# New order tables, filler tables and scheduler preferences for the attention half of a two-layer trunk

## The chip, the cores and the metric

The kernel runs on one core of a Trainium2 chip. The metric is the device time of one execution in microseconds (us); the smaller the better. TensorE (PE) does matrix products and transposes, VectorE (DVE) and ScalarE (ACT) work on tiles in SBUF and PSUM, GpSimd (POOL) helps DVE, and SyncE (SP) issues the DMAs. A difference under 0.5% (6.3 us here) is one that a measurement of this kernel does not tell from none.

## What is computed

Two layers, each an attention half and a feed-forward half on 512 tokens of width 1024, in float32:

```
h = rms_norm(x, attn_norm[l]);  proj = h @ w_in[l]
o_fox  = forgetting attention, 6 heads x 64:  softmax(q.k/8 + c[t] - c[s]) v
o_diff = differential attention, 4 heads:     (softmax(q1 k1) - lam softmax(q2 k2)) v, then rms_norm
o_dsa  = sparse attention, 6 heads x 64:      an indexer scores all keys, the top 128 of each row stay
x = x + concat(o_fox, o_diff, o_dsa) @ w_out[l]
h = rms_norm(x, ffn_norm[l]);  gate, up = split(h @ w_gate_up[l])
x = x + (silu(gate) * up) @ w_down[l]
```

All attention is causal. Every projection is made as three products (high x high, low x high, high x low) of operands split into a high part rounded to fp32r and a remainder.

## The kernel before

The attention half of a layer runs through 16 heads in one list: four differential heads (names with d), six forgetting heads (f), six sparse heads (s). A name reads kind, layer, pair of heads, head in the pair: f0_2_0 is layer 0, third pair of forgetting heads, first head. A head goes through stages: its queries and keys are transposed (tp_q, tp_k; ACT copies them out as T_q, T_k), scores are multiplied (s_), DVE adds the bias and takes the row minimum (x_ and st_, line 444, "ttr"), ACT takes the exponential (p_, line 445), PE transposes the weights (t_, line 456), ACT and DVE copy them out as high and low part (pt0 line 470, pt1 line 474), PE multiplies them with the values (o_), and at the end of a pair the rows are divided by their sums (osb, lines 513 and 518) and split (oh by ACT, ol by DVE).

The loop over rounds works on several heads at once: a round holds eleven stages, those of the scores of the next head, the transposes of this one, the products with the values of the last one. ORDER gives the order of the eleven in each round, a hexadecimal digit for each. After each stage, FILL says how many units of other PE work follow. A unit is taken from one queue (`fillers`): 12 matmuls of the projection chunks (pj), then 6 matmuls of the output projection of the differential heads (wo_diff), then 9 of the forgetting heads (wo_fox), then the sparse ones. SEARCH says how many steps of the top-128 search (DVE, lines 880 and 881) follow; INDEX_FILL does the same as FILL ahead of the first round.

PE runs in program order, so ORDER and FILL are its order. On DVE, ACT and POOL a scheduler sets the order at build time; `ahead(kind)` gives the instructions of a kind a preference, by the numbers in AHEAD (a larger one puts them further forward, a negative one back). At run time each engine takes its instructions strictly in the order so found; an instruction that waits for a semaphore holds up all behind it on its engine. PSUM tiles come from rings: "mm" three buffers (projections), "st" four (scores and transposes), "o" one. A matmul into a ring's buffer waits until the last reader of the tile before it there is done.

After the attention half, `split_input` (line 186 on) makes yh (ACT, line 192) and yl (DVE, line 195) of x for the feed-forward half; the first gate-and-up product gu0_0_0 (lines 958 to 960) takes them one by one.

```
for e, si in enumerate(ORDER[r + 1]):
    stages[int(si, 16)]()
    step(filler, int(FILL[r + 1][e]))
    if r <= 8:
        step(topk, int(SEARCH[r + 1][e]))
```

Of the kernel before, what the change touches and what calls it, by code (L numbers as in the profile page):

```python
# [17 lines left out]
P = 128  # L18
# [3 lines left out]
KT = D // P  # L22
# [9 lines left out]


ORDER = [
    "025314678a9", "0213457869a", "0213564789a", "1023647589a", "0312547698a", "1023465798a",
    "012435687a9", "0214365789a", "3021475698a", "0132645798a", "0123564879a", "021364587a9",
    "0132546798a", "1032546789a", "102345768a9", "103624758a9", "012345689a7", "012436587a9",
    "0362145897a",
]
FILL = [  # L40
    "10100011102", "01011000210", "10000011011", "01000011200", "00411000001", "00011010011",
    "02000002011", "00200040001", "00010101000", "10000000001", "00000000000", "01100000010",
    "00000000010", "00000000001", "00000000010", "00000000110", "00000000000", "00010100000",
    "01000000000",
]
SEARCH = [
    "00000000300", "00002010000", "00000000002", "11100004000", "00002000020", "00100000010",
    "00002001000", "20101020101", "01100001001", "02501140001",
]
INDEX_FILL = "03210121000201021"  # L50

AHEAD = {
    "bias": 300, "comb": 60, "dqh": -150, "dql": 150, "evac": 1000, "norm": 150, "oadd": 600, "osb": 60,
    "prep": 200, "raw": 300, "red": -150, "rl": 1000, "rope": 60, "rows": -60, "rt": 60, "sc": 1000,
    "split": -60, "sq": 200, "stack": 60, "tl": 300, "topk": 150, "ttr": 1000, "val": 300, "vall": 1000,
    "wl": 200, "yh": 300, "yl": 250, "ssq": -100, "post": 1000, "wh": 0, "fh": 200, "xadd": 1000,
}


# [29 lines left out]
def trunk(ctx: ExitStack, tc: tile.TileContext, x_in, w_in, w_out, w_gu, w_dn, vecs, gfeat, rope, out):  # L89
    nc = tc.nc  # L90
    V, A, G, T, SY = nc.vector, nc.scalar, nc.gpsimd, nc.tensor, nc.sync
# [17 lines left out]
    ahead = lambda kind: tc.high_priority(AHEAD[kind])  # L109
# [29 lines left out]
    dram = ctx.enter_context(tc.tile_pool(name="dram", bufs=1, space=bass.MemoryType.DRAM))  # L139


    def weights(src, n, step, name, eng=V, load=None, hi="wh"):

        raw = wp.tile([P, 1024], F32, tag="raw", name=f"raw_{name}", bufs=2)
        for o in range(0, n, load or n):
            SY.dma_start(raw[:, o:o + (load or n)], src[:, o:o + (load or n)])
        piece = n if n <= 512 else -(-n // step // 2) * step
        hs, ls = [], []
        for o in range(0, n, piece):
            w = min(piece, n - o)  # L150
            h = wp.tile([P, 512], F32R, tag="wh", name=f"wh_{name}_{o}")
            with ahead(hi):
                A.activation(h[:, :w], raw[:, o:o + w], AF.Copy)  # L153
            lo = wp.tile([P, 512], F32R, tag="wl", name=f"wl_{name}_{o}")
            with ahead("wl"):
                eng.tensor_tensor(lo[:, :w], raw[:, o:o + w], f32(h[:, :w]), op=ALU.subtract)  # L156
            hs.append(h)
            ls.append(lo)

        def part(a, b):  # L160
            e = a // piece
            return hs[e][:, a - e * piece:b - e * piece], ls[e][:, a - e * piece:b - e * piece]
        return part

    def mm3(ps, ah, al, bh, bl, first, last):
        T.matmul(ps, ah, bh, start=first, stop=False, skip_group_check=True)  # L166
        T.matmul(ps, al, bh, start=False, stop=False, skip_group_check=True)  # L167
        T.matmul(ps, ah, bl, start=False, stop=last, skip_group_check=True)  # L168
# [52 lines left out]
    def attention(l, ap):  # L221
# [56 lines left out]
        def step(gen, n):  # L278

            for _ in range(n):  # L280
                try:
                    next(gen)
                except StopIteration as e:
                    return e.value
# [138 lines left out]
        def key_stacks(hl, name, tag="qk", bufs=5):  # L423

            return [stacked(lambda b: flat(hl(b))[:, 64 * e:64 * e + 128], f"{name}{e}", tag, bufs) for e in range(2)]
# [429 lines left out]
        def index_queries(h):  # L855
            if h % 2 == 0:
                hl["i"] = ap.tile([P, NB, 2, 2, 64], F32R, tag="hl", name=f"hliq{l}_{h}", bufs=1)
                split_hl(raw0[:, :, h:h + 2], hl["i"], True)
            return stacked(lambda b: flat(hl["i"][:, b, h % 2]), f"iq{l}_{h}")

        def index_score(h, q, i):

            n = (i + 1) * P
            ps = st_tile(f"is{l}_{h}_{i}")
            for e in range(2):
                T.matmul(ps[:, :n], q[:, i * P:(i + 1) * P], ikT[e][:, :n], start=(e == 0), stop=(e == 1))
            rl = xt_tile(f"rl{l}_{h}_{i}")
            with ahead("rl"):
                A.activation(rl[:, :n], ps[:, :n], AF.Relu, scale=0.125)
            with ahead("sc"):  # L870
                V.scalar_tensor_tensor(sc[i], rl[:, :n], wi[:, i, h:h + 1], sc[i] if h else causal[:, S - n:],
                                       op0=ALU.mult, op1=ALU.add if h else ALU.subtract)
# [13 lines left out]

        step(filler, int(INDEX_FILL[0]))
        q = index_queries(0)
        for h in range(IDX):
            if h == 1:  # L890
                skT = key_stacks(lambda b: hlk[:, b, 1], f"sk{l}", "skT", 2)
            step(filler, int(INDEX_FILL[4 * h + 1]))
            nq = index_queries(h + 1) if h + 1 < IDX else None
            for i in range(1, NB):
                step(filler, int(INDEX_FILL[4 * h + 1 + i]))
                index_score(h, q, i)
# [39 lines left out]
    def feed_forward(l, fp):  # L936
# [9 lines left out]
        def gate_up(f, between=None):  # L946

            pgu = []
            for u in range(2):
                if u and between:  # L950
                    between()
                part = weights(w_gu[l, :, (2 * f + u) * KT * P:(2 * f + u + 1) * KT * P], KT * P, P, f"gu{l}_{f}_{u}", hi="fh")
                ps = (st_tile if u else mm_tile)(f"gu{l}_{f}_{u}")
                if f == 0 and u == 0:

                    for kt in range(KT):
                        wh, wl = part(kt * P, (kt + 1) * P)
                        T.matmul(ps, wh, y[kt][0], start=(kt == 0), stop=False, skip_group_check=True)
                        T.matmul(ps, wl, y[kt][0], start=False, stop=False, skip_group_check=True)
                    for kt in range(KT):  # L960
                        T.matmul(ps, part(kt * P, (kt + 1) * P)[0], y[kt][1], start=False, stop=(kt == KT - 1), skip_group_check=True)
                else:
                    for kt in range(KT):
                        mm3(ps, *part(kt * P, (kt + 1) * P), *y[kt], kt == 0, kt == KT - 1)
                pgu.append(ps)
            return pgu
# [50 lines left out]
        def split_sum(src, name, eng):  # L1017
            h = fp.tile([P, half], F32R, tag="wsh", name=f"wsh_{name}", bufs=5)
            with ahead("fh"):
                A.activation(h, src, AF.Copy)  # L1020
            lo = fp.tile([P, half], F32R, tag="wsl", name=f"wsl_{name}", bufs=5)
            with ahead("wl"):
                eng.tensor_tensor(lo, src, f32(h), op=ALU.subtract)  # L1023
            return h, lo

        def seven(f):

            raws, parts = [], {}
            for u in range(2):
                raw = (fp if u else wp).tile([P, 1024], F32, tag="raw", name=f"raw_gu{l}_{f}_{u}", bufs=2)  # L1030
# [10 lines left out]
            def whole(src, k):  # L1041
                h = wp.tile([P, 512], F32R, tag="wh", name=f"wh_gu{l}_{f}_{k}")
                with ahead("fh"):
                    A.activation(h, src, AF.Copy)
                lo = wp.tile([P, 512], F32R, tag="wl", name=f"wl_gu{l}_{f}_{k}")
                with ahead("wl"):
                    V.tensor_tensor(lo, src, f32(h), op=ALU.subtract)
                return h, lo

# [36 lines left out]
        def down(group, ms):  # L1086
            f0, f1 = DOWN_GROUPS[group]
            n = (f1 - f0) * P
            for m in ms:
                off = KT * P * f0 + m * n  # L1090
                part = weights(w_dn[l, :, off:off + n], n, P, f"dn{l}_{f0}_{m}")
                ps = mm_tile(f"dn{l}_{f0}_{m}")
                for e, f in enumerate(range(f0, f1)):
                    mm3(ps, *part(e * P, (e + 1) * P), gt[f][0], gt[f][1], f == f0, f == f1 - 1)
                V.tensor_tensor(x[m], ps, x[m], op=ALU.add)  # L1095
                if l == DEPTH - 1 and f1 == NF:
                    SY.dma_start(out[:, m, :], x[m])
# [99 lines left out]
```

## Time and profile before

| | us |
|---|---|
| median of 3 runs | 1262.66 (1261.4 to 1265.97) |
| the profiled execution, its own time | 1261.8 |
| its span | 1260.1 |
| PE busy | 1236.7 (98%) |
| DVE busy | 1012.4 (80%) |
| ACT busy | 741.7 (59%) |
| POOL busy | 248.7 (20%) |
| mean granted TensorE clock | 0.999 |

The profiled execution took 1.7 us outside its span, and its time lies 0.86 us below the median of the runs. Layer 0's attention half lies at about 43 to 289 us of the span, that of layer 1 at about 667 to 913 us. Times in the rows are counted from the start of the span. Where the profile merges buffer numbers, s_f stands for all score tiles of the forgetting heads.

### The profile page before, as it was taken

Reading aid. Unit: us, or ns where it says so; the run is one execution under the profiler, and the core shown is the slowest. Engines: PE = TensorE matmul, PEld = TensorE weight load, DVE = VectorE, ACT = ScalarE, POOL = GpSimd, SP = SyncE. Lnnn points to the kernel's source line nnn. Section 1 sums busy time; section 2 is a strip of 40 time slices with the busy share of each in tenths; the row PEclk is TensorE's granted clock in tenths of the full one; section 3 lists DMA queues with packets and bytes.
Section 4 is the critical chain, followed back from the end, with each engine's and each line's share of the span. In section 5 each row is a group of like instructions: output and inputs, shape, how many; then the busy total and the mean of one; then the engine's idle time right before and its main releaser. Section 6 shows DMA issues by size and latency. Waiting matters only on the chain. (4 is left out here: it accounts for less than half of the span.)

```text
span 1260.1 us, 22735 instructions
## 1 busy us (share of the span) xinstructions
PE 1236.7 (98%) x8366; PEld 1115.9 (89%) x8366; DVE 1012.4 (80%) x2345; ACT 741.7 (59%) x1686; POOL 248.7 (20%) x271
## 2 busy tenths in 40 slices
PE   9999999999999999999999899999999999999998
PEld 9988897788998998999899888968889989989997
DVE  5699996769985995998546999868699769959962
ACT  6679777867543552454456787778665435534531
POOL 1554466230000000000025545642200000000000
PEclk9999999999999999999999999999999999999999
DMA  5221221133323332422332212211333343234232
GB/s 188 85 77 51 60 77 47 39 109 100 117 80 108 117 104 81 135 84 68 97 88 79 82 51 59 72 34 60 105 101 115 91 115 113 82 92 127 75 99 84
DMA packets 34639, 111.76 MB, mean 89 GB/s; under 512 B 3952, under 2 KB 4448, under 8 KB 34528
## 3 DMA queue, kind: packets, MB, share of 16 engines
q1 hardware_dynamic: 34528, 110.31, 29.4%
q8 instruction: 66, 1.08, 0.3%
q14 instruction: 45, 0.37, 0.1%
HBM read 108.14 MB, written 2.15 MB: 88 GB/s over the span
## 5 line engine op out<-in xcount | busy, mean ns | idle before, releaser
L166 PE MATMUL pj<-wh_in,yh 128*128 128x256 f32 (+1 forms) x704 | 202.5, 288 | 0.4 <-ACT wh_in L153 0.4
L167 PE MATMUL pj<-wh_in,yl 128*128 128x256 f32 (+1 forms) x704 | 199.3, 283 | 0.0
L168 PE MATMUL pj<-wl_in,yh 128*128 128x256 f32 (+1 forms) x704 | 199.3, 283 | 0.0
L168 PE MATMUL dn<-gl,wh_dn 128*128 128x512 f32 x352 | 138.7, 394 | 0.0
L167 PE MATMUL dn<-gh,wl_dn 128*128 128x512 f32 x352 | 138.0, 392 | 0.0
L153 ACT ACTIVATE wh_dn<-raw_dn 128x512 fp32r<-128x512 f32 x96 | 57.1, 595 | 137.1 <-PE dn L168 106.5
L166 PEld LDWEIGHTS pj<-wh_in,yh 128*128 128x128 f32 x704 | 135.2, 192 | 2.5 <-issue 1.2
L166 PE MATMUL dn<-gh,wh_dn 128*128 128x512 f32 x352 | 136.6, 388 | 0.0
L167 PEld LDWEIGHTS pj<-wh_in,yl 128*128 128x128 f32 x704 | 135.4, 192 | 0.7
L168 PEld LDWEIGHTS pj<-wl_in,yh 128*128 128x128 f32 x704 | 135.3, 192 | 0.2 <-DVE wl_in L156 0.2
L1020 ACT ACTIVATE wsh<-ws 128x512 fp32r<-128x512 f32 x144 | 89.6, 630 | 70.9 <-PE gu_c L168 32.8
L156 POOL TENSOR_TENSOR wl_in<-raw_in,wh_in 128x512 fp32r<-128x512 f32 x72 | 98.8, 1389 | 107.1 <-ACT wh_in L153 102.6
L156 DVE TENSOR_TENSOR wl_dn<-raw_dn,wh_dn 128x512 fp32r<-128x512 f32 x96 | 61.7, 646 | 49.2 <-ACT wh_dn L153 48.3
L1023 DVE TENSOR_TENSOR wsl<-ws,wsh 128x512 fp32r<-128x512 f32 x144 | 97.6, 685 | 1.1 <-ACT wsh L1020 0.2
L167 PEld LDWEIGHTS dn<-gh,wl_dn 128*128 128x128 f32 x352 | 66.1, 188 | 15.2
L166 PEld LDWEIGHTS dn<-gh,wh_dn 128*128 128x128 f32 x352 | 66.1, 188 | 14.5
L168 PEld LDWEIGHTS dn<-gl,wh_dn 128*128 128x128 f32 x352 | 66.2, 188 | 13.1
L231 POOL MEMSET causal<- 128x512 f32 x2 | 1.1, 528 | 357.3 <-PE dn L168 357.3
L1095 DVE TENSOR_TENSOR x<-dn,x 128x512 f32<-128x512 f32 x48 | 32.8, 690 | 44.9 <-PE dn L168 44.9
L153 ACT ACTIVATE wh_in<-raw_in 128x512 fp32r<-128x512 f32 (+1 forms) x88 | 53.1, 625 | 23.4 <-PE pj L167 13.4
L881 DVE MATCH_REPLACE8 sc<-top,sc 128x384 f32<-128x384 f32 (+2 forms) x96 | 51.4, 537 | 0.0
L880 DVE MAX8 top<-sc 128x8 f32<-128x256 f32 (+2 forms) x96 | 50.8, 545 | 0.3
(397 smaller groups left out, 3950.1 us busy)
## 6 DMA issues: line engine op xcount, KB each, us to landing
raw_gu<-in_w_gu SPq DMA_DIRECT2D x88, 512.0 KB
raw_in<-in_w_in SPq DMA_DIRECT2D x39, 512.0 KB
raw_dn<-in_w_dn SPq DMA_DIRECT2D x32, 448.0 KB
raw_dn<-in_w_dn SPq DMA_DIRECT2D x16, 512.0 KB
cr<-rtd_c SPq DMA_DIRECT2D x12, 256.0 KB
raw_o_fox<-in_w_out SPq DMA_DIRECT2D x8, 384.0 KB
x<-in_x_in SPq DMA_DIRECT2D x8, 256.0 KB
raw_o_diff<-in_w_out SPq DMA_DIRECT2D x4, 512.0 KB
```

Of the source, the lines that this page charges most:

```text
L153: A.activation(h[:, :w], raw[:, o:o + w], AF.Copy)
L156: eng.tensor_tensor(lo[:, :w], raw[:, o:o + w], f32(h[:, :w]), op=ALU.subtract)
L166: T.matmul(ps, ah, bh, start=first, stop=False, skip_group_check=True)
L167: T.matmul(ps, al, bh, start=False, stop=False, skip_group_check=True)
L168: T.matmul(ps, ah, bl, start=False, stop=last, skip_group_check=True)
L231: G.memset(causal, 0.0)
L880: V.max(top, sc[i])
L881: V.match_replace(sc[i], top, sc[i], TAKEN)
L1020: A.activation(h, src, AF.Copy)
L1023: eng.tensor_tensor(lo, src, f32(h), op=ALU.subtract)
L1095: V.tensor_tensor(x[m], ps, x[m], op=ALU.add)
```

## The change

Five tables are replaced: ORDER, FILL, SEARCH, INDEX_FILL and AHEAD. The preference for splitting feed-forward weights gets a kind of its own, fl, with the old number of wl. No instruction is added or removed on any engine; the table that replaces ORDER is two lines shorter, so lines of the changed kernel are numbered two less. The layers use the same tables. A line or two of ORDER and FILL, and INDEX_FILL and AHEAD whole:

```diff
 ORDER = [
...
-    "0132546798a", "1032546789a", "102345768a9", "103624758a9", "012345689a7", "012436587a9",
-    "0362145897a",
+    "01234587a69", "103624758a9", "021345689a7", "1025473869a", "0132456897a",
 FILL = [
...
-    "02000002011", "00200040001", "00010101000", "10000000001", "00000000000", "01100000010",
+    "01100200101", "00010100000", "20000000100", "00000000001", "00000000000", "00000000010", "01000000001",
...
-INDEX_FILL = "03210121000201021"
+INDEX_FILL = "03400003001000221"
 AHEAD = {
-    "bias": 300, "comb": 60, "dqh": -150, "dql": 150, "evac": 1000, "norm": 150, "oadd": 600, "osb": 60,
-    "prep": 200, "raw": 300, "red": -150, "rl": 1000, "rope": 60, "rows": -60, "rt": 60, "sc": 1000,
-    "split": -60, "sq": 200, "stack": 60, "tl": 300, "topk": 150, "ttr": 1000, "val": 300, "vall": 1000,
-    "wl": 200, "yh": 300, "yl": 250, "ssq": -100, "post": 1000, "wh": 0, "fh": 200, "xadd": 1000,
+    "bias": 60, "comb": 60, "dqh": 0, "dql": 150, "evac": 100, "norm": 350, "oadd": -150, "osb": -100,
+    "prep": 300, "raw": 1000, "red": -150, "rl": 0, "rope": 0, "rows": -60, "rt": -150, "sc": 1100,
+    "split": -150, "sq": -150, "stack": 60, "tl": 250, "topk": 150, "ttr": 1050, "val": 0, "vall": 60,
+    "wl": 300, "yh": 0, "yl": 300, "ssq": 0, "post": 1000, "wh": 0, "fh": 200, "fl": 200, "xadd": 1050,
 }
...
-    def weights(src, n, step, name, eng=V, load=None, hi="wh"):
+    def weights(src, n, step, name, eng=V, load=None, hi="wh", low="wl"):
...
-            with ahead("wl"):
+            with ahead(low):
```

The other lines of the diff pass low="fl" for the feed-forward weights, or name "fl" in place of "wl" there.

What moves is seen best in the order of instructions. Numbers at the end of names are buffer instances and mean nothing here.

DVE in layer 0, round of head f0_2_0, before: the score tile s_f0_2_00_0 is read by the last row shown; ahead of it stand the division of osb_f0_0 by its row sums, the sums into x0, x1 and x2, and the preparation of the sparse heads' queries (rst_s, rn_s, raws, ra_s).

```order
L179 TENSOR_TENSOR rst_s0_2970<-rst_s0_2970,ss_s0_2954 128x24
L781 TENSOR_TENSOR x0_70<-wo0_diff_0_3055,x0_70 128x512
L180 TENSOR_SCALAR rst_s0_2970<-rst_s0_2970 128x24
L513 TENSOR_TENSOR osb_f0_0_2621<-osb_f0_0_2621,rw_f0_0_2596 128x512
L181 TENSOR_TENSOR rn_s0_2968<-rst_s0_2970,rsy_s0_2969 128x24
L336 TENSOR_TENSOR raws0_2705<-raws0_2705,rn_s0_2968 128x1536
L781 TENSOR_TENSOR x1_71<-wo0_diff_1_3084,x1_71 128x512
L406 TENSOR_TENSOR raws0_2705<-raws0_2705,gsq0_448 128x1536
L781 TENSOR_TENSOR x2_72<-wo0_diff_2_3109,x2_72 128x512
L342 TENSOR_TENSOR ra_s0_2979<-raws0_2705,rp_95 128x384
L444 ISA x_f0_2_00_0_3097,st_f0_2_00_3012<-s_f0_2_00_0_3092,fbf0_2_0_0_3030 128x128
```

The same place now, from the same first row on:

```order
L177 TENSOR_TENSOR rst_s0_2967<-rst_s0_2967,ss_s0_2951 128x24
L178 TENSOR_SCALAR rst_s0_2967<-rst_s0_2967 128x24
L179 TENSOR_TENSOR rn_s0_2965<-rst_s0_2967,rsy_s0_2966 128x24
L779 TENSOR_TENSOR x0_70<-wo0_diff_0_3036,x0_70 128x512
L334 TENSOR_TENSOR raws0_2675<-raws0_2675,rn_s0_2965 128x1536
L404 TENSOR_TENSOR raws0_2675<-raws0_2675,gsq0_448 128x1536
L779 TENSOR_TENSOR x1_71<-wo0_diff_1_3081,x1_71 128x512
L340 TENSOR_TENSOR ra_s0_2976<-raws0_2675,rp_95 128x384
L442 ISA x_f0_2_00_0_3094,st_f0_2_00_3006<-s_f0_2_00_0_3089,fbf0_2_0_0_3061 128x128
```

The division of osb_f0_0 has left this stretch (it now stands ahead of x_f0_1_10_0, a round earlier), and the sum into x2 stands behind the score rows. On PE, between s_f0_2_00_0 and the transposes t_f0_2_0_0 that need the result, two transposes of keys (tp_kf0_2_10 and _11) and two products o_f0_1_1 are put in; they stood right behind t_f0_2_0_0 before.

PE in layer 0, around the second part of the scores of head f0_0_0, before (the row ahead is the last matmul of a unit of chunk 8):

```order
L456 MATMUL t_d0_1_1_2_2204<-ident_80,p_d0_1_10_2_1964 128x128 x3
L456 MATMUL t_d0_1_1_3_2213<-ident_80,p_d0_1_10_3_2004 128x128 x4
L511 MATMUL rows_d0_0_2220<-ident_80,rw_d0_0_2058 128x128 x4
L482 MATMUL o_d0_1_0_2030<-pt0_d0_1_0_1802,vals0_1_116 64x256
L482 MATMUL o_d0_1_0_2030<-pt0_d0_1_0_1802,vals0_1_116 64x128
L438 MATMUL s_f0_0_00_2_2234<-T_kf0_0_00_2137,T_qf0_0_0_2027 128x384
L438 MATMUL s_f0_0_00_2_2234<-T_kf0_0_01_2144,T_qf0_0_0_2027 128x384
L438 MATMUL s_f0_0_00_3_2250<-T_kf0_0_00_2137,T_qf0_0_0_2027 128x512
```

Now:

```order
L454 MATMUL t_d0_1_1_2_2210<-ident_80,p_d0_1_10_2_1961 128x128 x3
L454 MATMUL t_d0_1_1_3_2219<-ident_80,p_d0_1_10_3_2001 128x128 x4
L509 MATMUL rows_d0_0_2226<-ident_80,rw_d0_0_2058 128x128 x4
L436 MATMUL s_f0_0_00_2_2236<-T_kf0_0_00_2137,T_qf0_0_0_2030 128x384
L436 MATMUL s_f0_0_00_2_2236<-T_kf0_0_01_2144,T_qf0_0_0_2030 128x384
L480 MATMUL o_d0_1_0_2014<-pt0_d0_1_0_1811,vals0_1_116 64x256
L480 MATMUL o_d0_1_0_2014<-pt0_d0_1_0_1811,vals0_1_116 64x128
L164 MATMUL pj0_8_1_2085<-wh_in0_8_1_0_2178,yh00_4_267 128x256
```

The products o_d0_1_0 stand behind the first scores now, and a unit of chunk 8 (12 matmuls) follows them ahead of s_f0_0_00_3. Ahead of the first row shown stands one more unit than before.

ACT at the end of layer 0's attention half, where x is split for the feed-forward half, before (sqx are the squares for the norm, wh_gu the high parts of weights, xg a scaled copy for later):

```order
L192 ACTIVATE yh10_4_4139<-x4_74,gf_78 128x512
L206 ACTIVATE sqx10_4_4166<-x4_74 128x512
L206 ACTIVATE sqx10_5_4169<-x5_75 128x512
L192 ACTIVATE yh10_5_4143<-x5_75,gf_78 128x512
L153 ACTIVATE wh_gu0_0_1_512_4220<-raw_gu0_0_1_4214 128x512
L206 ACTIVATE sqx10_6_4172<-x6_76 128x512
L153 ACTIVATE wh_gu0_1_0_0_4251<-raw_gu0_1_0_4249 128x512
L192 ACTIVATE yh10_6_4147<-x6_76,gf_78 128x512
L998 ACTIVATE xg0_4_4337<-x4_74,gf_78 128x512
L192 ACTIVATE yh10_7_4151<-x7_77,gf_78 128x512
L206 ACTIVATE sqx10_7_4175<-x7_77 128x512
```

Now:

```order
L204 ACTIVATE sqx10_4_4166<-x4_74 128x512
L996 ACTIVATE xg0_4_4337<-x4_74,gf_78 128x512
L204 ACTIVATE sqx10_5_4169<-x5_75 128x512
L151 ACTIVATE wh_gu0_0_1_512_4220<-raw_gu0_0_1_4214 128x512
L190 ACTIVATE yh10_4_4139<-x4_74,gf_78 128x512
L151 ACTIVATE wh_gu0_1_0_0_4251<-raw_gu0_1_0_4249 128x512
L204 ACTIVATE sqx10_6_4172<-x6_76 128x512
L190 ACTIVATE yh10_5_4143<-x5_75,gf_78 128x512
L204 ACTIVATE sqx10_7_4175<-x7_77 128x512
L190 ACTIVATE yh10_6_4147<-x6_76,gf_78 128x512
L190 ACTIVATE yh10_7_4151<-x7_77,gf_78 128x512
```

The last four yh rows have moved back; ahead of yh10_7 one instruction more than before stands, sqx10_7.

In the rounds of the first sparse heads (FILL from its row 12 on), the units wo_diff_6 and wo_diff_7 leave the round of head s0_0_0 and now stand in the two rounds after it; the units of wo_fox there move back by as much.

## Rows read from the trace of the kernel before

**Rows 1.** The page, busy time, share of the span and instructions of each engine.
```profile
PE 1236.7 (98%) x8366; PEld 1115.9 (89%) x8366; DVE 1012.4 (80%) x2345; ACT 741.7 (59%) x1686; POOL 248.7 (20%) x271
```
**Rows 2.** A window of layer 0: length, busy us per engine (instructions), clock, DMA.
```profile
140.00:180.00 40.00, 36.79 (x283) 32.99 (x282) 40.00 (x125) 27.23 (x77) 22.33 (x31) 1.00 0.20 58
```
**Rows 3.** What PE waited for: waiting, releasing instruction: us in total, times, longest.
```profile
PE s_d L438 <- DVE st_d L444: 3.1, 4, 1.2
...
PE s_f L438 <- DVE st_f L444: 2.1, 2, 1.0
...
PE s_f L438 <- ACT T_kf L418: 1.5, 2, 1.4
```
**Rows 4.** Timeline of PE, layer 0, second scores of f0_0_0: start, length, instruction, idle before.
```profile
145.38 0.86 PE L482 MATMUL o_d<-pt_d,vals 128*64 128x256 f32 x4
147.27 0.62 PE L438 MATMUL s_f<-T_kf,T_qf 128*128 128x384 f32 x2 [1.03 <-DVE st_f L444]
148.37 0.74 PE L438 MATMUL s_f<-T_kf,T_qf 128*128 128x512 f32 x2 [0.48 <-ACT pt_d L470]
```
**Rows 5.** Timeline of all engines, layer 0, first scores of head f0_1_0.
```profile
170.04 1.24 DVE L705 TENSOR_SCALAR om_d<-om_d 128x8 f32<-128x8 f32 x1
...
171.31 0.21 ACT L175 ACTIVATE rsy_d<-om_d 128x8 f32<-128x8 f32 x1 [3.29 <-DVE om_d L705]
171.43 1.07 ACT L418 ACTIVATE T_kf<-tp_kf 128x512 fp32r<-128x512 f32 x2
...
172.06 0.33 PE L438 MATMUL s_f<-T_kf,T_qf 128*128 128x128 f32 x1 [1.36 <-ACT T_kf L418]
```
**Rows 6.** Line 705 on DVE: durations in ns, least, median, greatest.
```profile
L705 DVE TENSOR_SCALAR om_d<-om_d x4: 151/154/1235, 135.1 to 790.9; 128x8 f32<-128x8 f32 x4
```
**Rows 7.** Timeline of all engines, layer 0, first transposes of head f0_2_0.
```profile
200.89 1.32 POOL L156 TENSOR_TENSOR wl_o_diff<-raw_o_diff,wh_o_diff 128x512 fp32r<-128x512 f32 x1 [3.93 <-ACT wh_o_diff L153]
200.97 1.79 DVE L513 TENSOR_TENSOR osb_f<-osb_f,rw_f 128x512 f32<-128x512 f32 x1
...
207.06 0.68 DVE L781 TENSOR_TENSOR x<-wo_diff,x 128x512 f32<-128x512 f32 x1
...
208.36 0.28 DVE L444 CUSTOM_DVE_ANT_0 x_f<-s_f,fbf 128x128 f32<-128x128 f32 x1
...
208.68 0.40 ACT L445 ACTIVATE p_f<-x_f,st_f 128x128 f32<-128x128 f32 x1 [1.72 <-DVE st_f L444]
...
209.22 0.33 PE L456 MATMUL t_f<-ident,p_f 128*128 128x128 f32 x1 [1.45 <-ACT p_f L445]
```
**Rows 8.** Timeline of PE, layer 1, the same transposes, of head f1_2_0.
```profile
831.93 0.33 PE L456 MATMUL t_f<-ident,p_f 128*128 128x128 f32 x1 [1.41 <-ACT p_f L445]
```
**Rows 9.** Window of layer 1 behind that wait, columns as in rows 2.
```profile
833.20:836.50 3.30, 3.30 (x11) 1.33 (x9) 1.51 (x4) 1.92 (x8) 3.22 (x5) 0.50 0.05 18
```
**Rows 10.** Timeline of PE, layer 0, rounds of heads s0_0_0 to s0_1_0.
```profile
224.07 0.49 PE L456 MATMUL t_s<-ident,p_s 128*128 128x128 f32 x3
...
230.35 0.73 PE L438 MATMUL s_s<-T_sk,T_qs 128*128 128x512 f32 x2 [0.37 <-DVE st_s L444]
230.92 0.39 PE L166 MATMUL wo_diff<-oh,wh_o_diff 128*128 128x512 f32 x1
...
232.31 0.60 PE L511 MATMUL rows_f<-ident,rw_f 128*128 128x128 f32 x4
233.03 0.52 PE L456 MATMUL t_s<-ident,p_s 128*128 128x128 f32 x3
...
239.24 0.49 PE L456 MATMUL t_s<-ident,p_s 128*128 128x128 f32 x3
...
245.31 0.49 PE L456 MATMUL t_s<-ident,p_s 128*128 128x128 f32 x3
```
**Rows 11.** Timeline of all engines, layer 0, start of the feed-forward half.
```profile
289.41 0.70 ACT L192 ACTIVATE yh<-x,gf 128x512 fp32r<-128x512 f32 x1
...
290.17 0.50 PE L958 MATMUL gu<-yh,wh_gu 128*128 128x512 f32 x1 [0.44 <-ACT yh L192]
```

More of the change, by code (lines that the diff above doesn't have):

```diff
@@ L34 @@
 ORDER = [
-    "025314678a9", "0213457869a", "0213564789a", "1023647589a", "0312547698a", "1023465798a",
-    "012435687a9", "0214365789a", "3021475698a", "0132645798a", "0123564879a", "021364587a9",
-    "0132546798a", "1032546789a", "102345768a9", "103624758a9", "012345689a7", "012436587a9",
-    "0362145897a",
+    "0235164789a", "021345786a9", "0213564789a", "3160245789a", "3012547869a", "0213547698a", "102435687a9",
+    "0132645987a", "30142758a69", "0231465798a", "1032456987a", "012365478a9", "0132546789a", "0125346798a",
@@ L39 @@
+    "01234587a69", "103624758a9", "021345689a7", "1025473869a", "0132456897a",
 ]
 FILL = [
-    "10100011102", "01011000210", "10000011011", "01000011200", "00411000001", "00011010011",
-    "02000002011", "00200040001", "00010101000", "10000000001", "00000000000", "01100000010",
-    "00000000010", "00000000001", "00000000010", "00000000110", "00000000000", "00010100000",
-    "01000000000",
+    "10010101102", "01101001100", "20001001011", "01000110200", "00412000012", "00010001011", "20000001101",
@@ L45 @@
+    "01100200101", "00010100000", "20000000100", "00000000001", "00000000000", "00000000010", "01000000001",
+    "00001000110", "00000000100", "00000000001", "00000100000", "00000010000",
 ]
 SEARCH = [
-    "00000000300", "00002010000", "00000000002", "11100004000", "00002000020", "00100000010",
-    "00002001000", "20101020101", "01100001001", "02501140001",
+    "01000000100", "11200001000", "00000000102", "00001003000", "10000000020", "00100200010", "01001001100",
+    "21010001000", "01011000001", "10521040021",
@@ L951, in gate_up @@
                     between()
-                part = weights(w_gu[l, :, (2 * f + u) * KT * P:(2 * f + u + 1) * KT * P], KT * P, P, f"gu{l}_{f}_{u}", hi="fh")
+                part = weights(w_gu[l, :, (2 * f + u) * KT * P:(2 * f + u + 1) * KT * P], KT * P, P, f"gu{l}_{f}_{u}", hi="fh", low="fl")
                 ps = (st_tile if u else mm_tile)(f"gu{l}_{f}_{u}")
@@ L1021, in split_sum @@
             lo = fp.tile([P, half], F32R, tag="wsl", name=f"wsl_{name}", bufs=5)
-            with ahead("wl"):
+            with ahead("fl"):
                 eng.tensor_tensor(lo, src, f32(h), op=ALU.subtract)
@@ L1045, in whole @@
                 lo = wp.tile([P, 512], F32R, tag="wl", name=f"wl_gu{l}_{f}_{k}")
-                with ahead("wl"):
+                with ahead("fl"):
                     V.tensor_tensor(lo, src, f32(h), op=ALU.subtract)
@@ L1090, in down @@
                 off = KT * P * f0 + m * n
-                part = weights(w_dn[l, :, off:off + n], n, P, f"dn{l}_{f0}_{m}")
+                part = weights(w_dn[l, :, off:off + n], n, P, f"dn{l}_{f0}_{m}", low="fl")
                 ps = mm_tile(f"dn{l}_{f0}_{m}")
```

## The prediction

> **What bounds the kernel now.** I read the page first: PE is busy 98% of the span [rows 1], and 1260.1 - 1236.7 = 23.4 us is all that PE idles. Nothing is added or taken away on any engine, so only PE's waits, its clock and what an order costs besides can change. Then the windows: in the attention half of layer 0, from 140 to 180 us, PE has 36.79 busy of 40.00, while DVE has 40.00 of 40.00 [rows 2]. There DVE is never short of work: search steps, which nobody needs for long, fill its queue, and PE waits when something it needs stands behind them. Then the waits of PE. Most scores of the differential heads wait for DVE (3.1 us in four waits) [rows 3]; on PE and DVE the order around these is the same before and after, so they stay. What the change touches is read from the timelines at four places, which are there in both layers.
>
> **The change part by part.**
>
> *Place A, second scores of f0_0_0 and first scores of f0_1_0.* PE waits 1.03 us for DVE and 0.48 for ACT at the first [rows 4], 1.36 for ACT at the second [rows 5]. A unit of projection has 12 x 256 columns, one of wo_diff 6 x 512, the same 3072, and a wo_diff unit takes 232.31 - 230.92 = 1.39 [rows 10]. At the first place one such unit now stands ahead of the scores and the four matmuls o_d0_1_0 (0.86 [rows 4]) go behind them: 1.39 - 0.86 = 0.53 us more cover, so the wait falls from 1.03 to 0.5; behind it 0.86 + 1.39 now lie between the two score tiles, and the 0.48 goes. That is about 1.0 us. But DVE sets the pace in this stretch, and PE only comes sooner to the next thing it waits for. At f0_1_0 the ACT queue is held by the rsy_d row, which waits 3.29 us for om_d0_1 on DVE; the keys T_kf stand right behind it [rows 5]. In the new order two more units of projection (2 x 1.39 = 2.8) are ahead of the scores there. DVE has three more instructions ahead of om_d0_1; between 0.28 and 0.68 each [rows 7], 0.8 to 2.0, I take 1.6. om_d0_1 itself took 1.24 where its median is 0.154 [rows 6]; if that does not come again, 1.1 is given back. On ACT, T_kf used to start 0.12 behind rsy_d; now a copy of projections, the second rsy_d (0.21) and one T_q (half of 1.07) stand between, about 1.2 with 0.4 for the copy. So the release comes later by 1.6 + 1.2 = 2.8, or 1.7 without the slow om, and PE's own work by 2.8: for both waits together nothing to 1.1 us is won in layer 0. I take 0.6. In layer 1 the second wait does not exist (the two waits for T_kf, 1.5 us, are the 1.36 and 0.16 of layer 0) while the first does (two waits for st_f, 2.1 us) [rows 3]; there the 1.0 of the first place and some 0.3 of smaller ones can stay won. A = -0.6 - 1.3 = -1.9; ends: -0.4 if DVE takes all back, -5.0 if every wait here goes (3.0 in layer 0, 2.0 in layer 1).
>
> *Place B, first transposes of head f0_2_0.* PE waits 1.45 us in layer 0 [rows 7] and 1.41 in layer 1 [rows 8] for ACT's p_f, and ACT for DVE's x_f, which began at 208.36. Ahead of it DVE now lacks the division of osb_f0_0 (1.79) and the sum into x2 (0.68): 2.47 less [rows 7]. The queries' norm also waits for ACT (rsy) at its start, so I take 1.9 of it. PE for its part does the keys' transposes and two o_f0_1_1 ahead of t_f0_2_0_0, work that was done right behind it. The wait of 1.45 plus a second of 0.16 is covered by the 1.9 alone: -1.6 a layer. The division is not free where it goes, ahead of x_f0_1_10_0, but that tile's weights are transposed only after two more projection units. B = -3.2; ends: 0, and -4.0, a quarter above the idle shown, since a stop also breaks the overlap of matmuls (an estimate).
>
> The 1.79 is itself worth a look: it began 0.08 behind a POOL instruction of 1.32 that reads the same kind of operands, while a sum of the same 512 columns takes 0.68 [rows 7]. The Trainium skill, page "SBUF — State Buffer", section "SBUF: two separate sides", says that a DVE instruction with two SBUF inputs and a GpSimd instruction that reads SBUF exclude each other, the one that starts first holding the shared port pair to its end. The row agrees: 1.79 - 0.68 = 1.1 lost. By that rule the new place of the division need not be cheaper, and any POOL split that starts ahead of raws now puts up to its own 1.32 in front of x_f; place B would then win 0.3 in place of 1.6.
>
> *Place C, rounds of the first sparse heads.* From the transposes of s0_0_0 to those of s0_0_1 PE takes 233.03 - 224.07 = 8.96 us, with two wo_diff units (2.8) in it; the next rounds take 6.21 and 6.07 [rows 10]. The change empties the first: 8.96 - 2.78 - 0.37 of wait = 5.8 stay. The second gets a wo_diff unit of six matmuls in place of a wo_fox unit of nine like ones (1.39 x 9/6 = 2.09): 6.21 - 0.70 = 5.5. These rounds are a chain of scores, DVE, ACT, transposes, ACT, values. No round without a filler of 1.39 or more is in the trace. The nearest is 6.07, with filler. If no round gets below that, the two cost 6.07 - 5.8 + 6.07 - 5.5 = 0.8; the units moved on cover smaller waits later, say 0.2. C = +0.6 a layer, +1.2. Ends: -0.5 a layer if the cover was not needed; +2.8 if the first round stays as long as it was and its units come on top later.
>
> *Place D, start of the feed-forward half.* ACT is without a break there, and PE waits 0.44 for yh10_7, which starts at 289.41 and takes 0.70 [rows 11]. One more instruction, sqx10_7 (512 columns, like yh10_7 under 0.70), now precedes it. PE has nothing else to do there: +0.6 a layer, D = +1.2; ends 0 and +1.4. yh10_4 to yh10_6 come later too, but by no more than this at the matmuls that use them one after the other.
>
> *Place E, the clock.* In layer 1, some 1.3 us behind the wait of 1.41, 3.30 us ran at 0.50, that is 1.2 GHz [rows 9]; layer 0 has an equal wait and no drop. At half speed 3.30 us hold half the work: up to 1.65 lost. If the wait goes, the drop may go with it; I take a bit more than a third, E = -0.6; ends -1.65 and +1.65 (another such drop).
>
> The rest costs nothing that I can find: feed-forward splits keep their preference (200 as fl), the search ends at the same row of DVE as before, ahead of the first sparse head, and the DMAs keep their order.
>
> **Sum.** -1.9 - 3.2 + 1.2 + 1.2 - 0.6 = -3.3. The profiled execution took 1261.8: 1258.5. It lies 0.86 below the median of the runs, so in their terms 1259.4. I forecast 1259.
>
> **The rivals.**
> 1. *Everything that can go, goes.* A -5.0, B -4.0, C -1.0, D 0, E -1.65: -11.7, about 1250.5. For it: fillers are put just where PE waited at A and B. Against it: DVE at 40.00 of 40.00 [rows 2] cannot be earlier, and D has an ACT without a gap.
> 2. *DVE gives nothing away, and the change does not do what it says.* A -0.4, B 0 (the exclusion of DVE and POOL, or a new collision, puts the 1.9 back), C +1.2, D +1.2, E 0: +2.0, about 1264. For it: the 1.79 and the 1.24 show how often a DVE row is late here [rows 6, 7].
> 3. *The emptied sparse rounds stall.* C +2.8 a layer; once a wait there gets to about the 1.4 us that came ahead of the drop in layer 1, the clock drops behind it, +1.65 a layer; A -0.4, B -3.2, D +1.2: 5.6 + 3.3 - 0.4 - 3.2 + 1.2 = +6.5, about 1269. For it: no round there ran without filler. Against it: waits seen there are 0.4 or less, and with a stop of 0.7 a round, as I reckon, there is no drop.
>
> **How the numbers follow.** The forecast has 0.45, rival 1 0.22, rival 2 0.20, rival 3 0.13. The range for 8 in 10 goes from 1251 to 1267; the forecast's own range is 1255 to 1262. A measurement of this kernel tells 0.5%, 6.3 us, from no change: faster is below 1256.4, slower above 1269. Faster: nearly all of rival 1 and a tail of the forecast, 0.27. Slower: half of rival 3 and what I have not seen, 0.12. Within: 0.61.
>
> **What would show it.** In the new profile: at A the DVE wait of about 0.5 at the second scores of f0_0_0, and one of 0.8 to 1.4 for T_kf at f0_1_0 in layer 0; at B no wait for p_f over 0.3; at C the two rounds at 6 us each and waits for st_s or pt_s that were not there; at D the wait for yh at 1.0 in place of 0.44; no window of layer 1's attention half below a clock of 1.00. Wrong would be: waits at A gone while DVE stays full (then DVE did not set the pace), a p_f wait over 1 us (B), a round s0_0_0 at 5.6 us or over 7 (C).

## The result

The changed kernel takes 1250.49 us (median of 4 runs, 1249.22 to 1250.89) against 1262.63: a ratio of 0.990, 95% interval 0.9884 to 0.9915. That is 12.1 us less, where 3.3 were forecast; it is within half a microsecond of the first rival's 11.7, and just below the lower end of the range. The profiled execution took 1250.89 with a span of 1249.2, 10.9 less than before.

The page after, as in [rows 1]: PE's idle time falls from 23.4 to 15.8 us, its busy time by 3.3. DVE does the same instructions in 5.9 us less, POOL in 10.4 less.

```profile
PE 1233.4 (99%) x8366; PEld 1114.6 (89%) x8366; DVE 1006.5 (81%) x2345; ACT 740.8 (59%) x1686; POOL 238.3 (19%) x271
```

To see where it came from, each matmul's start is set against the pace of all matmuls ahead of it (the usual start-to-start step of each kind, from the trace before). What a stretch takes beyond that pace is lost there. The level hangs on the step that is taken as usual; what is read is the difference between before and after:

| lost, us | layer 0 before | after | layer 1 before | after |
|---|---|---|---|---|
| first feed-forward work or start, to s_f0_0_00_0 | 12.2 | 12.4 | 6.2 | 5.9 |
| place A, to the scores of f0_1_1 | 5.2 | 0.9 | 3.9 | 0.9 |
| from there to the scores of f0_2_0 | 0.2 | 2.1 | 0.2 | 0.1 |
| place B with the clock, to t_s0_0_0_0 | 2.9 | 1.0 | 4.4 | 1.0 |
| place C, to the first gate-and-up product | 1.5 | 0.9 | 1.4 | 0.9 |
| place D, that product | 0.7 | 1.3 | 0.7 | 1.3 |

Place A after, all engines in layer 0, against [rows 4, 5]: no wait ahead of the second scores of f0_0_0, none ahead of the first of f0_1_0.

```profile
146.86 0.60 PE L436 MATMUL s_f<-T_kf,T_qf 128*128 128x384 f32 x2
...
168.75 0.38 DVE L703 TENSOR_SCALAR om_d<-om_d 128x8 f32<-128x8 f32 x1
...
169.16 0.21 ACT L173 ACTIVATE rsy_d<-om_d 128x8 f32<-128x8 f32 x1 [0.26 <-DVE om_d L703]
...
170.10 1.08 ACT L416 ACTIVATE T_kf<-tp_kf 128x512 fp32r<-128x512 f32 x2
...
171.22 0.71 PE L436 MATMUL s_f<-T_kf,T_qf 128*128 128x128 f32 x4
```

om_d0_1 ends at 169.13 in place of 171.28, though three more DVE instructions stand ahead of it in the kernel. DVE is as full as in [rows 2], while PE has no idle time at all; the window from 140 to 180 us after:

```profile
140.00:180.00 40.00, 40.00 (x321) 37.05 (x320) 39.96 (x135) 30.04 (x84) 24.36 (x33) 1.00 0.19 61
```

Place B after, against [rows 7]: the division takes 0.69 where it now stands, and PE's transposes follow without a wait, 2.5 us behind the start of the exponential.

```profile
189.21 0.69 DVE L511 TENSOR_TENSOR osb_f<-osb_f,rw_f 128x512 f32<-128x512 f32 x1
...
205.28 0.28 DVE L442 CUSTOM_DVE_ANT_0 x_f<-s_f,fbf 128x128 f32<-128x128 f32 x1
...
205.60 0.40 ACT L443 ACTIVATE p_f<-x_f,st_f 128x128 f32<-128x128 f32 x1 [2.16 <-DVE st_f L442]
...
208.09 0.88 PE L454 MATMUL t_f<-ident,p_f 128*128 128x128 f32 x6
```

With the wait, the drop of the granted clock in layer 1 [rows 9] is gone from this execution; from 700 to 900 us the clock is now 1.00:

```profile
700.00:900.00 200.00, 198.21 (x1346) 170.28 (x1345) 173.97 (x530) 159.32 (x448) 90.61 (x104) 1.00 0.23 68
```

Place C after, PE, against [rows 10]: the emptied round takes 6.30 us with one wait of 0.29, the next one 5.50.

```profile
220.01 0.52 PE L454 MATMUL t_s<-ident,p_s 128*128 128x128 f32 x3
...
225.35 0.63 PE L509 MATMUL rows_f<-ident,rw_f 128*128 128x128 f32 x4 [0.29 <-DVE st_s L442]
226.31 0.51 PE L454 MATMUL t_s<-ident,p_s 128*128 128x128 f32 x3
...
231.81 0.51 PE L454 MATMUL t_s<-ident,p_s 128*128 128x128 f32 x3
```

One loss is new, in layer 0 only: ACT's high part of a w_out weight, now ahead of T_kf, waits 2.19 us for its DMA; PE then waits for pt_f. ACT and PE after:

```profile
184.67 0.63 ACT L151 ACTIVATE wh_o_diff<-raw_o_diff 128x512 fp32r<-128x512 f32 x1 [2.19 <-DMA raw_o_diff<-in_w_out]
...
192.36 1.72 PE L480 MATMUL o_f<-pt_f,vals 128*64 128x512 f32 x4 [0.86 <-ACT pt_f L468]
```

### The profile page after: what moved, and what is told of

The parts are those of the page before. It is cut to its first block, busy times and chain, and to the rows that moved or that the text cites. A ratio compares the mean times of both kernels' runs of the same rounds, so it can differ in the third digit from the quotient of the medians.

```text
span 1249.2 us, 22746 instructions
## 1 busy us (share of the span) xinstructions
PE 1233.4 (99%) x8366; PEld 1114.6 (89%) x8366; DVE 1006.5 (81%) x2345; ACT 740.8 (59%) x1686; POOL 238.3 (19%) x271
## 4 chain that ended last, share of the span: by engine, by line
PE 89%; DVE 6%; ACT 3%; issue 1%; DMA 1%; POOL 0%; SPq 0%; ACTq 0%; POOLq 0%; DVEq 0%
PE dn L166 7%; PE dn L165 6%; PE dn L164 6%; PE pj L164 6%; PE pj L166 5%; PE pj L165 5%; PE gu_d L164 3%; PE gu_a L164 3%; PE gu_a L165 3%; PE gu_d L166 3%; PE gu_d L165 3%; PE gu_a L166 3%; PE gu_c L164 3%; PE gu_c L165 3%; PE gu_c L166 3%; PE gu L164 2%
## 5 line engine op out<-in xcount | busy, mean ns | idle before, releaser
L154 POOL TENSOR_TENSOR wl_in<-raw_in,wh_in 128x512 fp32r<-128x512 f32 x72 | 94.5, 1327 | 122.2 <-ACT wh_in L151 101.3
L878 DVE MAX8 top<-sc 128x8 f32<-128x384 f32 (+2 forms) x96 | 51.8, 549 | 0.3
```

What stands on the lines that cost most here:

```text
L878: V.max(top, sc[i])
```

## The experiments

The question was which part of the change won, and why place A did not give back what it won. Each run edits one of the two kernels; its ratio, with a 95% interval, is to the kernel before, timed beside it.

**Tables or preferences.** e1 is the changed kernel with AHEAD as before, e2 the one with the four other tables as before.

> The changed kernel with the numbers of AHEAD as before (fl 200): only PE's order and the search steps are new. Theory T (the tables cover PE's waits, the preferences add little): 1252 to 1255, no wait over 0.6 at the second scores of f0_0_0, and place B (transposes of f0_2_0) covered in part. Theory P (the scheduler's order on DVE, ACT and POOL brought most of it): 1258 to 1262, with the waits at f0_0_0 or f0_1_0 still over 1 us.

1250.96 us, ratio 0.9916 (0.9902 to 0.9929).

> The changed kernel with ORDER, FILL, SEARCH and INDEX_FILL as before: only the preferences are new. Theory T: 1260 to 1265, the waits at f0_0_0 and f0_2_0 as in the kernel before (1.0 and 1.4 us). Theory P: 1252 to 1256, these waits under 0.5.

1260.69 us, ratio 0.9991 (0.9982 to 1.0000). So the tables alone bring 10.7 us, the preferences alone 1.0, which is at the edge of the interval; the whole change brought 12.1. e1 does better than either theory had it. But e2's trace is a surprise: with PE's order as before, the loss at place A falls from 5.2 to 1.5 in layer 0 (from 3.9 to 3.1 in layer 1); of PE's waits for st_f there, one of 0.11 us is left. Place B stays. e2's waits of PE:

```profile
PE t_f L456 <- ACT p_f L445: 3.2, 4, 1.4
...
PE s_f L438 <- ACT T_kf L418: 0.4, 2, 0.3
```

**The tables in three blocks**, each put into the kernel before: rows 0 to 7 and INDEX_FILL (e5), rows 8 and 9 (e6), rows 10 to 18 (e7). The filler units of each block sum to the same before and after.

```diff
-    "02000002011", "00200040001", "00010101000", "10000000001", "00000000000", "01100000010",
+    "02000002011", "00200040001", "00010100000", "20000000100", "00000000000", "01100000010",
```

(FILL of e6; ORDER and SEARCH likewise.)

> The kernel before with rows 0 to 7 of ORDER, FILL and SEARCH and INDEX_FILL of the change (index phase to the round of head f0_1_0), all else as before. Theory T (PE's order covers place A and nothing is taken back): place A gives 4.3 us in layer 0 and 2.0 to 3.0 in layer 1, so 1254 to 1257; the waits at f0_0_0 and f0_1_0 under 0.3, those at f0_2_0 (1.4) still there. Theory of the prediction (DVE sets the pace and takes most back): 1259 to 1261.

1257.25 us, 0.9964 (0.9950 to 0.9978), a quarter of a microsecond above the range of Theory T and outside that of the other. In its trace PE's waits at place A are 0.4 us in layer 0 and 0.2 in layer 1, and those at f0_2_0 are still there.

> The kernel before with rows 8 and 9 of ORDER, FILL and SEARCH of the change (rounds of the last two forgetting heads ahead of and at f0_2_0), all else as before. If place B is a matter of what PE does between the scores and the transposes of f0_2_0: 1.7 us a layer and up to 1.6 for the drop of the clock in layer 1, 1257 to 1259, no wait for p_f over 0.3. Rival (the division of osb on DVE has to move too, which the other rows or the preferences do): 1261 to 1262, the p_f wait over 0.8.

1257.95 us, 0.9968 (0.9958 to 0.9979). The four divisions of osb_f by row factors that a DMA brings (rw_f) are back at 0.68 each, and PE does not wait for p_f any more:

```profile
L513 DVE TENSOR_TENSOR osb_f<-osb_f,rw_f x4: 678/682/689, 188.7 to 840.6; 128x512 f32<-128x512 f32 x4
```

> The kernel before with rows 10 to 18 of ORDER, FILL and SEARCH of the change (rounds of the sparse heads), all else as before. From the two traces: 0.57 us a layer won between the first transposes of s0_0_0 and the end, so 1260.5. The prediction's term was 0.6 a layer lost: 1262.8.

1261.26 us, 0.9996 (0.9984 to 1.0008): by its interval neither a gain nor a loss is shown. The three medians lie 4.96 + 4.26 + 0.95 = 10.2 us below the kernel before, near e1's 10.7: the blocks add up as far as these runs can tell.

**The emptied rounds alone**, e4:

```diff
-    "00000000000", "00000000010", "01000000001",
+    "01100000000", "00000000000", "00000000001",
```

> The changed kernel with the units wo_diff_6 and wo_diff_7 back in the round of head s0_0_0, taken out of the two rounds behind it. Theory of the prediction (rounds without filler cost 0.6 a layer net): 1249.3. Theory 2 (emptied rounds are not the limit, their waits are 0.45 in all; the units are worth more in the later rounds): 1250.5 to 1252, with waits for st_s back at the rounds of s0_0_1 and s0_1_0.

1253.97 us, 0.9937 (0.9925 to 0.9950), 3.5 us slower than the changed kernel. The round of s0_0_0 loses the same 0.7 with or without the units; the two rounds behind it, now without them, lose 2.2 us in layer 0 against 0.1.

**The start of the feed-forward half**, e3: "yh" at 300 again.

> The changed kernel with the preference of yh at 300 as before. If the later yh rows cost 0.58 us a layer at the start of the feed-forward half (start to start 1.30 against 0.72), this gives 1.2 back: 1249.3. Rival: what precedes on ACT (the squares) then comes later and is waited for elsewhere, 1250.5 to 1251.5.

1248.74 us, 0.9897 (0.9882 to 0.9912): the median is 1.75 below that of the changed kernel, and the lowest of the versions that keep all arithmetic, but the intervals of the two ratios overlap. What shows the gain is the trace: the start of the feed-forward half is back at 0.65 a layer.

**Cover on PE**, e13: the round of f0_0_0 in the kernel before gets the changed order and three units more. Side by side, that round's strings of ORDER and FILL, and the string of FILL two rounds later that gives the units up:

```diff
-"0312547698a"     "00411000001"     "02000002011"
+"3012547869a"     "00412000012"     "02000000001"
```

> The kernel before with the round of f0_0_0 alone changed on PE: the products o_d0_1_0 behind the scores s_f0_0_00_2 and three units more in that round, which leave the round two later, behind its first scores. SEARCH and AHEAD as before. If PE's cover is what removed the waits at place A: 1.5 to 3 us a layer, 1257 to 1259, no wait at f0_0_0. If DVE takes back what PE wins (the prediction): under 1 us a layer, 1261, the wait for T_kf at f0_1_0 longer than 1.36 in layer 0.

1264.48 us, 1.0024 (1.0014 to 1.0034), slower. The waits at the second scores of f0_0_0 and, but for 0.16 us, at the first of f0_1_0 are gone. Others come at the sums (oss_d) and transposes ahead of f0_1_0, for DVE's st_f: 1.85 us in layer 0 and 1.66 in layer 1, where PE waited 0.18 and nothing before. Both layers together:

```profile
PE oss_d L701 <- DVE st_f L444: 2.2, 2, 1.2
...
PE t_f L456 <- DVE st_f L444: 1.3, 2, 0.7
```

In layer 0 the waits at place A fall from 3.2 to 2.3 us in all, but 3.4 us at a granted clock of 0.50 follow from 169.6 on, behind the wait of 1.25; in layer 1, without such a drop, they rise from 2.1 to 3.1. The loss there is 6.3 and 6.0 us, against 5.2 and 3.9 before. So PE's waits moved to the next scores that DVE has to read, and this cover was paid back. It is not a test of PE alone: the scheduler set DVE's order anew, with six more search instructions and two low parts pt_f fewer ahead of om_d0_1, and which of the two took the gain back is not shown. Together with e2, where PE's order stayed and the waits went, it says that DVE set the pace at place A.

**Taking the reads of GpSimd's subtractions away**, e8, in the kernel before: the low parts of these weights are left out of the result. The orders on PE, DVE and ACT stay the same row for row.

```diff
-                eng.tensor_tensor(lo[:, :w], raw[:, o:o + w], f32(h[:, :w]), op=ALU.subtract)
+                if eng is G:
+                    G.memset(f32(lo[:, :w]), 0.0)
+                else:
+                    eng.tensor_tensor(lo[:, :w], raw[:, o:o + w], f32(h[:, :w]), op=ALU.subtract)
```

> The kernel before, in which GpSimd writes zeros for the low parts of the weights of projection chunks 2 to 10 and of w_out in place of subtracting (it reads no SBUF there; the low parts are left out of the result). The orders of PE, DVE and ACT are the same row for row. Theory C (DVE rows are stretched where GpSimd holds what both read through, and that makes the waits at f0_0_0 and f0_1_0): the rows of 1.66, 0.99, 1.45 and 1.24 on DVE fall to their usual 0.75, 0.57, 0.68 and 0.15, DVE gets to these scores up to 3 us sooner, the waits at place A fall from 3.0 to under 1.5 in layer 0, 1256 to 1259. Theory O (only the order of PE counts): 1261 to 1263 with the waits as before.

1246.34 us, 0.9880 (0.9866 to 0.9894). 15.9 us, more than Theory C had. At place A, where PE waited 3.2 us in layer 0 and 2.1 in layer 1, it does not wait at all, with PE's order as before. DVE busy falls by 23.9 us for the same instructions:

```profile
PE 1230.4 (99%) x8366; PEld 1113.2 (89%) x8366; DVE 988.5 (79%) x2345; ACT 742.4 (60%) x1686; POOL 156.9 (13%) x271
```

How it works is seen at one instruction, the last sum of p_d for head d0_1 on DVE (128x512). The kernel before: a subtraction on POOL began at 136.00 (the row holds two of them; the first ended at 137.30), DVE's sum 0.19 later, and it took 1.66: it ended 0.55 behind that subtraction.

```profile
136.00 3.00 POOL L156 TENSOR_TENSOR wl_in<-raw_in,wh_in 128x512 fp32r<-128x512 f32 x2 [6.64 <-ACT wh_in L153]
136.19 1.66 DVE L633 SCALAR_TENSOR_TENSOR p_d<-p_d,st_d,p_d 128x512 f32<-128x512 f32 x1
```

The changed kernel: DVE began at 135.53, ahead of POOL's 136.02, and took 0.75. e8 took 0.74. After, then e8:

```profile
135.53 0.75 DVE L631 SCALAR_TENSOR_TENSOR p_d<-p_d,st_d,p_d 128x512 f32<-128x512 f32 x1
136.02 2.67 POOL L154 TENSOR_TENSOR wl_in<-raw_in,wh_in 128x512 fp32r<-128x512 f32 x2 [2.54 <-PE pj L165]
```
```profile
133.39 0.74 DVE L636 SCALAR_TENSOR_TENSOR p_d<-p_d,st_d,p_d 128x512 f32<-128x512 f32 x1
```

**Is it POOL's reads or its speed?** e12 writes each tile three times, so that POOL is busier than before.

> The kernel before with GpSimd writing the same zeros three times in a row in place of subtracting (1.6 us in place of 1.3 to 2.0; it reads no SBUF; low parts left out of the result). It keeps GpSimd as busy as before. Theory C (what DVE loses is lost to GpSimd's reads): as with one write, 1246 to 1248, DVE busy near 989. Rival (the gain of the one write came from GpSimd being done sooner, or its writes hold DVE up as well): 1253 or more, DVE busy over 1000.

1246.04 us, 0.9881 (0.9865 to 0.9898). DVE is as quick as in e8, with POOL at 260.5 us:

```profile
PE 1230.9 (99%) x8366; PEld 1113.7 (89%) x8366; DVE 987.2 (79%) x2345; ACT 741.8 (60%) x1686; POOL 260.5 (21%) x487
```

**The same edit in the changed kernel**, e10.

> The changed kernel, in which GpSimd writes zeros for the low parts of the weights of projection chunks 2 to 10 and of w_out in place of subtracting (the low parts are left out of the result). If the change won by meeting GpSimd less often on DVE and what is left still costs, this is faster than the changed kernel by 4 to 8 us (1243 to 1247), and its distance to the same edit of the kernel before (1246.3) is small, under 4 us. If the change won by PE's order alone, the two edits together add up: 12 us under 1246.3, 1234.

1245.62 us, 0.9871 (0.9857 to 0.9884). Without these reads, old and new tables with old and new preferences are 0.7 us apart, not 12; their intervals overlap. So nearly all that the change wins is won from what these subtractions cost. Whether it wins by meeting the reads less often or by covering the waits they make, this run does not tell: taking the reads away ends both. DVE and ACT do not have quite the order of the changed kernel here, since the scheduler set it anew.

**Moving reads away from POOL with all arithmetic kept**, e11: the low parts of w_out's weights are made by DVE (G, GpSimd, becomes V, VectorE, in three calls), with yh at 300.

> The changed kernel with yh at 300, and with the low parts of w_out's weights made by DVE in place of GpSimd (18 instructions a layer of about 0.6 us, 11 us of DVE, in rounds where DVE has 6 us of 20 free). Theory C: the DVE rows of 1.7 to 2.4 us there are no longer stretched, it gains 0.5 to 1.5 us against yh at 300 alone (1248.7): 1247.5. Rival: the added DVE work falls on the latency of the sparse rounds: 1250 to 1253.

1249.23 us, 0.9901 (0.9887 to 0.9914): no better than e3. At place B the loss falls from 1.0 to 0.7 in layer 0, but the sparse rounds lose 0.8 more, with new waits for rr_s.

## Why the prediction was wrong

- *Place A, the step that failed.* It is the walk along DVE's order with durations taken as fixed: I let three more instructions cost 1.6 us and gave 1.1 back for the slow om_d0_1 in one case only, so that DVE took back nearly all that PE won. DVE's durations are not fixed. Against the shortest one of each kind (same operation, tiles and shape, in the traces of before, after and e8), the DVE rows from the last scores of d0_1 to the first of f0_1_0 are longer by 7.0 us in layer 0 and 6.1 in layer 1 before, by 4.3 and 4.0 after, by 2.7 and 2.4 in e8 (e13, which lost: 6.1 and 6.0). So om_d0_1 ended 2.1 us sooner in layer 0, 0.7 of it already won at the last scores of d0_1, and not 0.5 to 1.6 later. The term was -1.9; A and the stretch behind it measured -5.5, even with the new 1.9 us of the DMA wait in layer 0, which the prediction had put at nothing ("the DMAs keep their order"; 13 of the 279 that SyncE issues stand at another place).
- *What held of it.* That DVE sets the pace there held (e2, e13). The prediction's own sign against it, waits gone while DVE stays full, did come (39.96 of 40.00), but it proves nothing: a row that is held up counts as busy. I took 40.00 of 40.00 for a sign that nothing could be won; in e8 the same window has 38.51.
- *The rows were there.* 1.24 against 0.154 [rows 6] and 1.79 against 0.68 [rows 7] are both gone in e8:

```profile
L708 DVE TENSOR_SCALAR om_d<-om_d x4: 152/155/163, 132.3 to 777.9; 128x8 f32<-128x8 f32 x4
...
L516 DVE TENSOR_TENSOR osb_f<-osb_f,rw_f x4: 685/688/689, 193.8 to 830.0; 128x512 f32<-128x512 f32 x4
```

  I used the Trainium skill's rule (page "SBUF — State Buffer", section "SBUF: two separate sides": a DVE instruction in a 2-port mode or with two SBUF inputs, the latter only against a GpSimd instruction that reads SBUF, and a GpSimd instruction shut each other out, the first holding the ports to its end) for place B alone, and as a reason for a loss. e8 and e12 agree with it: DVE's time falls by 23.9 and 25.2 us when the subtractions' reads go, and POOL's writes, 159 us of its time in e12, do not bring it back. om_d has one tensor input, and the trace does not show whether it ran in a 2-port mode; it shows that the slow one ended at 171.28, 0.03 behind a subtraction that ran on POOL from 169.54 to 171.25.
- *Not fewer meetings everywhere.* The changed kernel has new ones at other places: the four divisions of osb_s, 0.68 each before, are now slow, and ss_s takes 1.18 in place of 0.18. Its DVE is 18.0 us busier than e8's, and it is still only some 4 us slower: most of what DVE loses there costs PE nothing.

```profile
L513 DVE TENSOR_TENSOR osb_s<-osb_s,rw_s x4: 672/680/682, 251.6 to 889.4; 128x512 f32<-128x512 f32 x4
```
```profile
L511 DVE TENSOR_TENSOR osb_s<-osb_s,rw_s x4: 1197/1420/1620, 247.8 to 878.2; 128x512 f32<-128x512 f32 x4
```

- *Place B* was right in place and sign. Predicted with the clock -3.8, measured -5.2. e6 shows that two rows of the tables do it; there PE has its work between, and the division no longer takes 1.8, both at once. e8, with PE's order as before, leaves a wait of 0.15 a layer, so the quicker DVE alone does most of it.
- *The clock:* -0.6 against some 1.5 in the two traces, the difference of the layers at place B before (4.4 and 2.9). Of the profiled executions, the five that keep the p_f waits of 1.4 to 1.5 us (before, e2, e5, e7, e13) have drops to 0.50 inside the two attention halves, 3.4 us each: seven behind the ten such waits, three behind waits for st_f of 1.0 to 1.25 us. The other profiled executions have none there. The profiled execution of before, with one drop and a mean clock of 0.999, was a mild one: 48 more of that kernel lie at 0.996 to 0.999, 35 of them at 0.997 or less, and the 22 at 0.996 took 1262.6 us in the mean, the nine at 0.999 1260.9. The changed kernel's lie at 0.999 to 1.000. So the clock is likely a larger part of the 12.1 than the two traces show; how large is open. Nor does losing the p_f wait settle it: six of e6's eight executions are at 0.998, five of e2's eleven at 1.000.
- *Place C* was wrong in sign: +1.2 predicted, -1.1 in the two traces. The step was "If no round gets below that", that is 6.07: the second round took 5.50, while the first took 6.30 and loses the same 0.7 us filled or not. The units were worth more one and two rounds later (e4).
- *Place D* was right: +1.2 predicted, +1.1 in the traces, and in e3's trace it is gone.
- *A reading that was wrong without harm.* PE's order around the scores of the differential heads is not the same before and after: units move there too. That stretch loses the same, 12.2 and 12.4 in layer 0, 6.2 and 5.9 in layer 1.
- *Rival 1* named the same places, and the objection to it ("DVE at 40.00 of 40.00 cannot be earlier") was the fault. That its 11.7 is so near to 12.1 is in part luck: it had D at 0 where +1.1 was measured, and it did not have the new DMA wait; A without that wait won 7.3, more than its 5.0.

What stays open: e8, e10 and e12 also let POOL's instruction start without waiting for ACT, and free the raw weights sooner (the DMA wait of layer 0 is gone in e10); how much of their 16 us this is was not tried apart. How the 7.3 us of place A divide between cover on PE, a new order on DVE and shorter rows on DVE is not shown either. And why the new tables meet POOL's reads at other places is not shown beyond the single rows; where a POOL instruction starts follows from ACT and PE's releases of buffers, and nothing in the tables speaks of it.

## What to carry to other kernels

When an engine is full in the windows, check first that its instructions take their usual time: compare the least, median and greatest duration of a line, and look at what GpSimd ran when the greatest came. A walk along an in-order queue with median durations hides that. Cover put on PE ahead of one wait can be paid back at the next, if the engine that sets the pace does not get quicker (e13); a filler is worth most where its round has nothing else to do while the chain runs (e4: 3.5 us). And look at the granted clock of every execution, not only of the profiled one.

## What the runs showed of the hardware that was not expected

Without the reads of GpSimd's 108 subtractions for the low parts of weights (72 of wl_in and 36 for w_out, 146 us of its busy time in the kernel before) the kernel is 16 us of 1262 quicker, though GpSimd is busy 20% of the span, and DVE is 24 us less busy. Instructions as small as 128x8 are stretched eightfold (0.154 to 1.24 us). At the 331st matmul, ahead of any difference between the orders of before and of e7 on any engine, the one profiled execution was at 44.40 us and the other at 42.78; the same order can differ by 1.6 us there, so a single profile does not tell less than that.
